# Layer 0 of a two-layer decoder trunk: all column chunks of w_in over four parts of K, with the attention moved behind them

## The chip, the cores and the metric

The kernel runs on one core of a Trainium2 chip. The metric is the device time of one execution in microseconds. The kernel before took 2464.14 us (median of 3 runs, 2459.02 to 2468.23).

## The reference

Two layers on 256 tokens of width 2048, all float32. A layer normalizes x, scales and shifts it by values that come from a vector c through `w_mod`, multiplies by `w_in` (2048 x 5900 columns), runs three kinds of attention over the projections (4 MoBA heads, 4 NSA heads with two softmax branches and one compressed branch each, 8 FoX heads), multiplies by `w_out`, and then runs an MLP of squared ReLU.

```
mod = silu(c) @ w_mod + b_mod           # six groups of 2048 columns a layer
h = rms_norm(x, g_pre_mix) * (1 + scale) + shift
p = h @ w_in                            # q, k, v of MoBA; q, k, v, gates of NSA; q, k, v, forget of FoX
o = concat(moba(p), nsa(p), fox(p))     # 16 heads of 128
x = x + gate * rms_norm(o @ w_out, g_post_mix)
x = x + gate2 * mlp(modulated rms_norm(x))
```

FoX adds to each score the running sum of log sigmoid(forget); the compressed branch of NSA runs k and v blocks of 32 tokens through a small MLP with a GELU first.

## The kernel before, in words

Every product is made of three TensorE products: ScalarE casts a weight block to a shortened float (`hi`, L233), VectorE subtracts to get the rest (`lo`, L234), and TensorE multiplies hi by hi, hi by lo and lo by hi (`gemm_b`, L238 to L252). The block is a `unit` (L221): one transfer of 4 K tiles of 128 rows by up to 512 columns, 1 MiB, and 24 matmuls of 128x512. `chunk_a` (L265) makes the transposed form for FoX's q and k, 64 pairs of matmuls, 16 for each unit. Weights arrive in a ring of four 1 MiB buffers (`raw`).

The modulation `w_mod` is 16 MiB for each of six groups a layer. `mod_chunk` (L120) does it in one of two ways: VectorE multiplies and adds 1024 columns at a time (L148), or TensorE multiplies 512 columns of four K tiles at once (L143) and VectorE or ScalarE sums the result (L150 to L152). `Spread` (L189) lets a step of this work follow after each unit or head, at a rate given by R0 or MO; `tick` (L209) does that, and steps of the NSA compression (`comp`) come before it. Where `ring` holds names of big buffers, the w_mod blocks go into them, otherwise they share `raw`. The instruction order of each engine is fixed when the kernel is built, and an engine takes its instructions strictly in that order.

Layer 0 has four parts of K (q = 0 to 3), so that TensorE starts when a quarter of h is there. In each part, two 512-column chunks add up in PSUM (`pq`), and six more chunks (1024, 2048, 1536 and three of 344 columns) rotate through two PSUM banks: `rotate` (L558) sums them in SBUF, by ScalarE copy in part 0 and VectorE add (L572) later. Modulation groups 1 and 0 are made on TensorE beside the parts. After the last part come the four MoBA heads, the chunk of 268 columns with the NSA compression, FoX q and k of four heads by `chunk_a`, 8 softmax heads of NSA, 4 FoX heads, FoX q and k of the other four, their heads, and `w_out` in two halves of two column chunks. The boundary to the MLP (residual, normalization, transposes) follows. Layer 1 uses whole chunks and no parts.

A head (`softmax_head` L423) is scores (L431, L434; FoX also L433, L436, L437), mask and maximum (L443, L445), exp (L447), gate or reciprocal, three transposes (L455), a copy to SBUF (L457) and the product with v (L461, L462), which `put_split` writes (L465, L466). `to_heads` (L468) turns a projected chunk into heads: copy or add, rope, transposes (L484), copy (L485). `compress` (L494) multiplies blocks of raw compression weights (L506), copies to `hp`, transposes them (L514), makes the GELU and multiplies by the second weights (L528).

Of the kernel before, what the change touches and what calls it, by code (L numbers as in the profile page):

```python
# [20 lines left out]
NC = 15  # L21
NEG = -1e30
PES = (0, 1)
R0 = 48.5
MO = (3,3,4,5,5,5,5)
ROT = 6
CB = True
EXTRA = (7,)
# [4 lines left out]
G0 = ((0, 4), (0, 2), (0, 3))  # L33
# [3 lines left out]
AFD = ()  # L37
HIA = False
RA = (("S3", 1), ("", 1))
RB = ()  # L40
# [6 lines left out]
def trunk(ctx, tc, x, c, positions, w_mod, b_mod, g_pre_mix, g_post_mix, g_pre_mlp, g_post_mlp, w_in, b_forget,  # L47
# [56 lines left out]
    for l in range(DEPTH):  # L104
        stage = wk.tile([128, 128], F32, tag="P", name="stage", bufs=3)
        dma(stage[:96], b_mod[l].rearrange("(r k) -> r k", k=128))
        tp = ps_t()
        T.transpose(tp[:, :96], stage[:96], ident[:96, :96])
        V.tensor_copy(bm[:, l], tp[:, :96])

# [98 lines left out]
    def tick(w=1.0):  # L209
        if w == 1.0 and comp[0] is not None:  # L210
            if next(comp[0], 0) is None:
                if CB:
                    return
            else:
                comp[0] = None
# [104 lines left out]
    def norm_tile(h, l, which, r, t, q):  # L320
# [6 lines left out]
        for j in range(4):  # L327
            k = 4 * q + j
            if j in AFD:
                last[1] = V.tensor_scalar(hf[:, j], tp[:, j * 128:(j + 1) * 128], ac[:, k:k + 1], sh[:, k:k + 1],  # L330
                                op0=OP.mult, op1=OP.add)
            else:
                last[0] = A.activation(hf[:, j], tp[:, j * 128:(j + 1) * 128], AF.Identity, bias=sh[:, k:k + 1],
                             scale=ac[:, k:k + 1])
        ht = h[q // 2][:, 4 * q % 8:4 * q % 8 + 4, :, t * 128:(t + 1) * 128]
        if HIA:
            A.copy(ht[:, :, 0], hf)
        else:
            V.tensor_copy(ht[:, :, 0], hf)
# [32 lines left out]
    posi = cp.tile([128, 2], I32, name="posi")  # L372
    dma(posi, positions.rearrange("b (t p) -> p (b t)", p=128))
    posf = cp.tile([128, 2], F32, name="posf")
    V.tensor_copy(posf, posi)
    ang = cp.tile([128, 2, 16], F32, name="ang")
    for t in range(2):
        V.tensor_scalar(ang[:, t], invf, posf[:, t:t + 1], None, op0=OP.mult)
    sc = cp.tile([128, 2, 2, 16], F32, name="sc")
    C1 = 6.28125  # L380
    C2 = 0.001934051513671875
    C3 = 2.0 * math.pi - C1 - C2
    PI = 3.1415925
    for i, off in enumerate((0.25, 0.0)):
# [523 lines left out]
```

## Time and profile before

| | |
|---|---|
| median of 3 runs | 2464.14 us |
| profiled execution, span | 2459.2 us |
| TensorE busy | 2376.0 us (97%) |
| VectorE busy | 1648.0 us (67%) |
| ScalarE busy | 1210.9 us (49%) |
| mean granted TensorE clock | 0.986 |

The span runs from the first instruction to the last of the one profiled execution; the median of the runs lies 4.9 us above it. In the trace, layer 0 starts its first w_in matmul at 44.9 us, leaves the third part at 209 us, and ends w_out at 535.5 us; the boundary to the MLP then lasts to 557 us. TensorE is busy nearly all the time, so a stretch is read by how much of it TensorE waits and by what it has to do in it.

### The profile page before, as it was taken

How to read it: one execution, taken by the hardware profiler on the slowest of the kernel's cores; microseconds unless marked ns; L12 is line 12 of the kernel's file. 1: busy time of each engine (PE TensorE's matmuls, PEld its weight loads, DVE VectorE, ACT ScalarE, POOL GpSimd, SP SyncE). 2: the span in 40 equal slices, each digit the busy share in tenths (PEclk: the TensorE clock that was granted, in tenths of full speed). 3: DMA queues.
4: the chain of work that ended last, by engine and by line, in shares of the span. 5: the costliest groups of instructions: out<-in, count | busy, mean ns of one | idle time of the engine just before them, and what ended most of it. 6: DMA issues, size and time to landing. Idle time of an engine off the chain costs nothing.

```text
span 2459.2 us, 32050 instructions
## 1 busy us (share of the span) xinstructions
PE 2376.0 (97%) x12444; PEld 1977.0 (80%) x12444; DVE 1648.0 (67%) x2255; ACT 1210.9 (49%) x2025; POOL 12.9 (1%) x20
## 2 busy tenths in 40 slices
PE   5999999989999999999989999999999999999998
PEld 3678777778888888888878879887788888888886
DVE  3459688887777777777668467765665665665555
ACT  3435454455545535535545455544654553553553
POOL 0000000000000000000000000000000000000000
PEclk8999999999999999999999999999999999999999
DMA  9788888987888888888657588865567666666553
GB/s 348 284 327 309 300 293 297 349 296 244 296 296 281 309 304 278 311 277 308 199 199 273 188 276 306 282 244 180 176 227 234 222 237 225 221 205 198 187 189 120
DMA packets 292120, 632.83 MB, mean 257 GB/s; under 512 B 10608, under 2 KB 44800, under 8 KB 291712
## 3 DMA queue, kind: packets, MB, share of 16 engines
q1 hardware_dynamic: 291968, 630.79, 74.3%
q8 instruction: 97, 1.59, 0.3%
q14 instruction: 55, 0.45, 0.1%
HBM read 628.65 MB, written 2.10 MB: 256 GB/s over the span
## 4 chain that ended last, share of the span: by engine, by line
PE 88%; DVE 4%; DMA 4%; ACT 2%; issue 1%; POOL 0%; SPq 0%; DVEq 0%; POOLq 0%; ACTq 0%
PE psg L276 17%; PE psg L248 14%; PE psg L249 14%; PE psg L250 14%; PE psg L278 8%; PE psu L276 6%; PE psu L278 3%; PE psr L249 2%; PE psr L250 1%; PE psr L248 1%; PE pst L143 1%; PE pst L177 1%; DMA raw<-in_w_in_dram 1%; PE pst L325 1%; DMA rawm<-in_w_mod_dram 1%
## 5 line engine op out<-in xcount | busy, mean ns | idle before, releaser
L234 DVE TENSOR_TENSOR lo<-raw,hi 128x1024 fp32r<-128x1024 f32 (+2 forms) x784 | 928.6, 1191 | 582.3 <-ACT hi L233 580.8
L233 ACT CAST hi<-raw 128x1024 fp32r<-128x1024 f32 (+2 forms) x784 | 798.5, 1026 | 923.6 <-PE psg L250 468.3
L276 PE MATMUL psg<-S,hi 128*128 128x512 f32 x1888 | 674.3, 398 | 1.5 <-ACT hi L233 1.2
L248 PE MATMUL psg<-hi,S 128*128 128x512 f32 (+2 forms) x1664 | 640.1, 386 | 3.4 <-ACT hi L233 1.8
L249 PE MATMUL psg<-lo,S 128*128 128x512 f32 (+2 forms) x1664 | 638.4, 384 | 1.2 <-DVE lo L234 1.2
L250 PE MATMUL psg<-hi,S 128*128 128x512 f32 (+2 forms) x1664 | 637.5, 383 | 1.1 <-DVE S L340 1.1
L278 PE MATMUL psg<-S,lo 128*128 128x256 f32 x1888 | 528.6, 282 | 1.1 <-DVE lo L234 1.1
L276 PEld LDWEIGHTS psg<-S,hi 128*128 128x128 f32 x1888 | 355.1, 188 | 86.4 <-ACT hi L233 2.3
L248 PEld LDWEIGHTS psg<-hi,S 128*128 128x128 f32 x1664 | 312.5, 188 | 69.8 <-issue 4.2
L249 PEld LDWEIGHTS psg<-lo,S 128*128 128x128 f32 x1664 | 313.2, 188 | 61.8 <-DVE lo L234 3.1
L250 PEld LDWEIGHTS psg<-hi,S 128*128 128x128 f32 x1664 | 313.0, 188 | 61.2 <-DVE S L340 2.1
L278 PEld LDWEIGHTS psg<-S,lo 128*128 128x128 f32 x1888 | 357.1, 189 | 4.8 <-DVE lo L234 2.9
L148 DVE SCALAR_TENSOR_TENSOR acc<-rawm,cact,acc 128x1024 f32<-128x1024 f32 x226 | 289.2, 1280 | 16.6 <-DMA rawm<-in_w_mod_dram 14.7
L276 PE MATMUL psu<-S,hi 128*128 128x512 f32 x672 | 244.1, 397 | 0.0
L278 PE MATMUL psu<-S,lo 128*128 128x256 f32 x672 | 188.2, 280 | 0.0
L276 PEld LDWEIGHTS psu<-S,hi 128*128 128x128 f32 x672 | 126.2, 188 | 30.9 <-ACT hi L233 0.2
L278 PEld LDWEIGHTS psu<-S,lo 128*128 128x128 f32 x672 | 126.8, 189 | 0.3 <-issue 0.2
L249 PE MATMUL psr<-lo,S 128*128 128x512 f32 (+1 forms) x192 | 69.7, 363 | 1.5 <-DVE lo L234 1.5
L248 PE MATMUL psr<-hi,S 128*128 128x512 f32 (+1 forms) x192 | 68.5, 364 | 0.8 <-ACT hi L233 0.8
L250 PE MATMUL psr<-hi,S 128*128 128x512 f32 (+1 forms) x192 | 69.0, 359 | 0.0
L812 ACT ACTIVATE xu<-xu 128x256 f32<-128x256 f32 x128 | 52.6, 412 | 26.1 <-DVE xu L811 26.1
L325 PE MATMUL pst<-dg,xt 128*128 128x128 f32 x256 | 45.0, 342 | 20.9 <-DVE dg L317 19.9
(186 smaller groups left out, 1545.4 us busy)
## 6 DMA issues: line engine op xcount, KB each, us to landing
raw<-in_w_up_dram SPq DMA_DIRECT2D x128, 1024.0 KB, 5.3
raw<-in_w_down_dram SPq DMA_DIRECT2D x128, 1024.0 KB, 5.2
rawm<-in_w_mod_dram SPq DMA_DIRECT2D x119, 1024.0 KB, 6.0
raw<-in_w_in_dram SPq DMA_DIRECT2D x72, 1024.0 KB, 6.8
S<-in_w_mod_dram SPq DMA_DIRECT2D x16, 2048.0 KB, 11.0
raw<-in_w_out_dram SPq DMA_DIRECT2D x32, 1024.0 KB, 6.2
X<-in_w_mod_dram SPq DMA_DIRECT2D x26, 1024.0 KB, 7.3
raw<-in_w_in_dram SPq DMA_DIRECT2D x24, 688.0 KB, 6.2
```

The costliest lines, as they stand in the source:

```text
L143: T.matmul(pm[32 * k:32 * k + 32], cs.to_broadcast([128, 32]), raw[:, k], start=True, stop=True, tile_position=(0, 32 * k))
L148: V.scalar_tensor_tensor(acc, raw[:, k], cs, acc, op0=OP.mult, op1=OP.add)
L177: T.matmul(ps[:, j:j + 1], acc[:, j * 128:(j + 1) * 128], ones[:, 0:1], start=True, stop=True)
L233: A.copy(hi[:, :, :w], r)
L234: V.tensor_tensor(lo[:, :, :w], r, f32(hi[:, :, :w]), OP.subtract)
L248: T.matmul(ps[t][:, :w], xh, hi, start=first, stop=False)
L249: T.matmul(ps[t][:, :w], xh, lo, start=False, stop=False)
L250: T.matmul(ps[t][:, :w], xl, hi, start=False, stop=last)
L276: T.matmul(ps[d], hi[:, kk, ws], a.rearrange("p s n -> p (s n)"), start=(u == 0 and h == 0 and kk == 0), stop=False)
L278: T.matmul(ps[d][:, :256], lo[:, kk, ws], a[:, 0], start=False, stop=last)
L325: T.matmul(tp[:, j * 128:(j + 1) * 128], xt[:, t, k * 128:(k + 1) * 128], r, start=True, stop=True)
L812: A.activation(u, u, AF.Relu)
```

## The change

- Layer 0 rotates four FoX q and k chunks (columns 2828 on, 512 each) and the 268-column chunk too, in all four parts; their sums are in a big buffer `F` (`fac`), in `ack` and `vn`. They use the plain form of `gemm_b` and are turned by `to_heads`, where `chunk_a` produced the transposed form directly.
- In the last part the order is: MoBA's q, k, v; the four FoX chunks into `M`; the MoBA heads; the chunks 2048 and 268; the gates; 1536 with the compression; three of 344; then NSA, the forget gate's logarithm, all eight FoX heads, and w_out.
- w_out walks K outside and the two column chunks inside, in both layers.
- Modulation groups 1 and 0 alone stand beside parts 0 to 2 (before, one unit of the rest was drawn in with each); groups 4, 2, 3 all follow from the last part on, and group 2 is made on TensorE.
- At the start, the first w_mod transfers are issued before those of biases, positions and tables, and the work for those follows the first modulation units.
- Layers have their own big tags (S0, S1, F, M); in layer 1 this is a renaming.

The core of the diff:

```diff
-    def mod_groups(*lg):
+    def mod_groups(*lg, pe=()):
         for l, g in lg:
-            for q in range(2):
-                yield from mod_chunk(l, g, q, 1024)
+            if g in pe:
+                for q in range(4):
+                    yield from mod_chunk(l, g, q, 512, pe=True)
+            else:
+                for q in range(2):
+                    yield from mod_chunk(l, g, q, 1024)
...
+            gen = mod_first(0, (("M", 2), ("F", 2), ("S1", 2), ("", 1), ("", 1)))
+            for _ in range(3):
+                next(gen)
+            load_biases()
+            next(gen)
+            dma(xt, x.rearrange("b (t p) d -> p (b t) d", p=128))
+            for _ in gen:
+                pass
+            load_tables()
...
                 if q < 3:
-                    spread[0] = Spread(mod_both(q + 1), 8 + len(EXTRA), MO[ROT])
+                    spread[0] = Spread(mod_first(q + 1, (("M", 2), ("S1", 2)) if q < 2 else (("M", 2), ("", 1), ("", 1))),
+                                       8, MO)
                 else:
-                    ring[0] = RA
-                    spread[0] = Spread(rest, 48 - 3 * len(EXTRA), R0)
+                    spread[0] = Spread(mod_groups((0, 4), (0, 2), (0, 3), pe=(2,)), 48, R0)
...
+                if q < 3:
+                    for i in range(4):
+                        rotate(q, 2828 + 512 * i, 512, [fac[:, i]])
+                    for i in range(2):
+                        rotate(q, (2048, 1536)[i], 512, [ac2[:, i]])
+                    rotate(q, 2560, 268, [ack[:, :, 0:128], vn[:, :, 640:768], ack[:, :, 128:140]])
+                else:
+                    qfm = big("M", [128, 2, 8, 256], F32)
+                    qfs.extend([qfm[:, 0], qfm[:, 1]])
+                    for i in range(4):
+                        kind, gr = i // 2, i % 2
+                        to_heads(rotate_last(2828 + 512 * i, 512), qfs[gr], range(4 * kind, 4 * kind + 4), None, acc=fac[:, i])
+                    oT.append(big(TS["o"][0], [128, 8, 2, 256]))
+                    moba()
+                    to_heads(rotate_last(2048, 512), qk, range(4, 7), slice(0, 3, 2), vcopy=[(vn[:, :, 512:640], 384, 128)],
+                             acc=ac2[:, 0])
+                    ps = rotate_last(2560, 268)
...
+                    gate_values([ack[:, t, 128:140] for t in range(2)])
+                    comp[0] = compress_both(l, qk, load_w2(), cres)
+                    to_heads(rotate_last(1536, 512), qk, range(0, 4), slice(0, 4), acc=ac2[:, 1])
+                for i in range(3):
+                    rotate(q, 4876 + 344 * i, 344, [vt[:, :, 688:1024], lf] if i == 2 else [vt[:, :, 344 * i:344 * i + 344]])
...
+            ring[0] = RA
+            nsa()
+            log_forget()
+            ring[0] = ()
+            oT.append(big(TS["o"][1], [128, 8, 2, 256]))
+            fox_attn(0)
+            fox_attn(1)
...
         for pair in range(2):
             pp = [[ps_g(), ps_g()] for _ in range(2)]
-            for i in range(2):
-                for u in range(3):
+            for u in range(3):
+                for i in range(2):
                     gemm_b([(otile, Wo, 4 * u, 4 * u, (2 * pair + i) * 512, 512, pp[i], u == 0, False)])
```

In the changed kernel the same operations carry other lines: the three products are L236 to L238, hi L221, lo L222, TensorE's w_mod L128, VectorE's w_mod L133, a head's operations L423 to L458, the compression L498, L506, L520, and the add of `rotate` L667.

The order of TensorE at the first compression, before. L506 is a compression group, L514 the transposes of its result, L276 and L278 the FoX matmuls of `chunk_a`.

```order
L506 MATMUL pst<-rawc,tx 16x256 x8
L514 MATMUL pst<-cst,hp 128x15 x2
L276 MATMUL psg<-S_149,hi 128x512 x4
L278 MATMUL psg<-S_149,lo 128x256
L276 MATMUL psg<-S_149,hi 128x512
L278 MATMUL psg<-S_149,lo 128x256 x2
L276 MATMUL psg<-S_149,hi 128x512
```

The same place after. L498 is the compression group, L506 the transposes of its result, L520 the second weights, L580 the compressed scores, L423 the first NSA head's scores.

```order
L238 MATMUL psr<-hi,S_1446 128x344
L498 MATMUL pst<-rawc,tx 16x256 x8
L506 MATMUL pst<-cst,hp 128x15 x2
L520 MATMUL pst<-xg,w_2734 128x15 x2
L498 MATMUL pst<-rawc,tx 16x256 x32
L580 MATMUL spc<-kcmp,X_117 128x15 x8
L423 MATMUL pss<-X_117 128x128
L426 MATMUL pss<-X_117 128x256
```

What stood beside the compression of k and v (FoX matmuls) now stands far ahead of it; the k chain's three steps follow each other, then the groups of v, then NSA.

The order of TensorE in the FoX heads, before: L455 are a head's transposes, L461 its product with v, L276 and L278 the FoX matmuls of the second group.

```order
L276 MATMUL psg<-S_149,hi 128x512
L455 MATMUL pst<-cst,P 128x128
L278 MATMUL psg<-S_149,lo 128x256
L276 MATMUL psg<-S_149,hi 128x512
L455 MATMUL pst<-cst,P 128x128 x2
L278 MATMUL psg<-S_149,lo 128x256
L276 MATMUL psg<-S_149,hi 128x512
L278 MATMUL psg<-S_149,lo 128x256
L276 MATMUL psg<-S_149,hi 128x512
L461 MATMUL pst<-PT,X_160 128x256
```

After, in the FoX heads: L447 are the transposes, L453 and L454 the product with v, L423 to L429 the next scores, L128 modulation group 2.

```order
L128 MATMUL pst<-rawm,cact 32x512 x4
L429 MATMUL pss<-cst,lu 128x256
L447 MATMUL pst<-cst,P 128x128 x3
L423 MATMUL pss<-M 128x128
L453 MATMUL pst<-PT,X_119 128x256
L454 MATMUL pst<-PT,X_119 128x128
L128 MATMUL pst<-rawm,cact 32x512 x4
L425 MATMUL pss<-cst,lu 128x128
L426 MATMUL pss<-M 128x256
```

Between a head's steps there are now scores of the next head and a modulation group; matmuls of a weight unit come only at the last head, 9 of the 384 of w_out.

The order of VectorE in the MoBA heads, before: L443 and L445 are mask and maximum, L148 the modulation, L234 the `lo` of a weight unit.

```order
L443 ISA P,mx<-pss,cst 128x128
L443 ISA mx 128x1
L443 ISA P,mx<-pss,cst 128x256
L443 ISA mx 128x1
L234 TENSOR_TENSOR lo<-raw,hi 128x2x268
L445 TENSOR_SCALAR mx<-mx 128x2
L148 SCALAR_TENSOR_TENSOR acc<-S_1958,cact,acc 128x1024
L443 ISA P,mx<-pss,cst 128x128
L443 ISA mx 128x1
L148 SCALAR_TENSOR_TENSOR acc<-S_1958,cact,acc 128x1024
```

After: L435 and L437 are mask and maximum, L133 the modulation, L440 the reciprocal, L458 the write of a head, L222 the `lo` of the 2048 chunk.

```order
L435 ISA P,mx<-pss,cst 128x128
L435 ISA mx 128x1
L133 SCALAR_TENSOR_TENSOR acc<-rawm,cact,acc 128x1024
L458 TENSOR_TENSOR F<-pst,F 128x256
L435 ISA P,mx<-pss,cst 128x256
L435 ISA mx 128x1
L133 SCALAR_TENSOR_TENSOR acc<-rawm,cact,acc 128x1024
L440 RECIPROCAL sm<-sm 128x2
L437 TENSOR_SCALAR mx<-mx 128x2
L133 SCALAR_TENSOR_TENSOR acc<-rawm,cact,acc 128x1024
L458 TENSOR_TENSOR F<-pst,F 128x256
L222 TENSOR_TENSOR lo<-raw,hi 128x1024
```

Before, a `lo` of the next weight unit came among the second head's operations; now it comes at the end of the third, behind seven modulation operations (L133).

## Rows read from the trace of the kernel before

**Rows 1.** Busy times by stretch; columns named in its second line
```profile
core 0 of [0], span 2459.2 us
core 0: us, PE busy (x) PEld busy (x) DVE busy (x) ACT busy (x) POOL busy (x), PEclk, DMA share, GB/s
44.90:209.00 164.10, 158.39 (x866) 116.89 (x867) 91.68 (x124) 63.93 (x98) 0.00 (x0) 0.99 0.85 306
209.00:253.10 44.10, 44.08 (x238) 37.54 (x236) 42.34 (x78) 21.05 (x30) 0.00 (x0) 1.00 0.84 308
253.10:268.50 15.40, 13.71 (x89) 11.82 (x89) 14.49 (x43) 11.20 (x36) 0.00 (x0) 1.00 0.98 330
280.00:283.00 3.00, 0.69 (x16) 0.12 (x4) 1.70 (x12) 2.96 (x9) 0.00 (x0) 0.99 1.09 353
283.00:286.50 3.50, 3.39 (x9) 2.40 (x10) 2.25 (x7) 2.24 (x4) 0.00 (x0) 0.50 1.06 377
342.90:370.90 28.00, 22.52 (x126) 16.38 (x124) 26.20 (x92) 21.11 (x68) 0.00 (x0) 1.00 0.83 301
428.00:535.50 107.50, 103.53 (x484) 84.65 (x484) 88.35 (x116) 48.05 (x82) 0.55 (x1) 1.00 0.94 344
```

**Rows 2.** Timeline, start: us, duration, engine, line, out<-in, count, idle before
```profile
4.54 0.38 SPq L134 DMA_DIRECT2D S<-in_w_mod_dram  x1
...
34.61 3.64 PE L143 MATMUL pst<-S,cact 128*32 128x512 f32 x16 [1.77 <-DMA S<-in_w_mod_dram]
```

**Rows 3.** Timeline of TensorE inside a part of K
```profile
96.81 0.32 PE L248 MATMUL psr<-hi,S 128*128 128x344 f32 x1
...
101.26 0.32 PE L250 MATMUL psr<-hi,S 128*128 128x344 f32 x1
...
107.73 1.06 PE L143 MATMUL pst<-S,cact 128*32 128x512 f32 x8
...
109.29 0.40 PE L250 MATMUL psg<-hi,S 128*128 128x512 f32 x1
...
114.07 0.39 PE L250 MATMUL psg<-hi,S 128*128 128x512 f32 x1
```

**Rows 4.** Lines by form: count, busy us, mean ns, idle before and releaser
```profile
L234 DVE TENSOR_TENSOR lo<-raw,hi 128x1024 fp32r<-128x1024 f32 x720 | 876.7, 1223 | 556.6 <-ACT hi L233 555.2 <-PE pst L462 0.4
...
L148 DVE SCALAR_TENSOR_TENSOR acc<-rawm,cact,acc 128x1024 f32<-128x1024 f32 x226 | 289.2, 1280 | 16.6 <-DMA rawm<-in_w_mod_dram 14.7
...
L177 PE MATMUL pst<-cst,acc 128*128 128x1 f32 x256 | 31.1, 249 | 4.9 <-DVE acc L152 4.9
...
L484 PE MATMUL pst<-cst,ev 128*128 128x128 f32 x64 | 10.7, 279 | 1.0 <-DVE ev L407 0.8
...
L572 DVE TENSOR_TENSOR X<-psr,X 128x512 f32<-128x512 f32 x6 | 4.1, 689 | 2.8 <-PE psr L250 2.8
```

**Rows 5.** Timeline of ScalarE: table loads between the softmax of MoBA and the gates
```profile
269.00 1.28 ACT L744 ACT_TABLE_LOAD   x1
...
279.81 1.28 ACT L676 ACT_TABLE_LOAD   x1
```

**Rows 6.** Timeline of the first compression
```profile
279.63 1.06 PE L506 MATMUL pst<-rawc,tx 128*16 128x256 f32 x16
...
283.07 1.03 PE L514 MATMUL pst<-cst,hp 128*128 128x15 f32 x4 [2.38 <-ACT hp L511]
...
289.56 0.61 PE L528 MATMUL pst<-xg,w 128*128 128x15 f32 x4
```

**Rows 7.** Timeline of ScalarE: copies that end a head's transposes
```profile
348.87 0.48 ACT L457 COPY PT<-pst 128x384 f32<-128x384 f32 x1 [0.52 <-PE pst L455]
...
367.89 0.46 ACT L457 COPY PT<-pst 128x384 f32<-128x384 f32 x1
...
436.06 0.48 ACT L457 COPY PT<-pst 128x384 f32<-128x384 f32 x1 [0.53 <-PE pst L455]
...
448.74 0.48 ACT L457 COPY PT<-pst 128x384 f32<-128x384 f32 x1
```

More of the change, by code (lines that the diff above doesn't have):

```diff
@@ L103, in trunk @@
     bm = cp.tile([128, DEPTH, 96], F32, name="bm")
[L104 to L109, printed above, removed]
     xt = cp.tile([128, 2, D], F32, name="xt")
@@ L328, in norm_tile @@
             k = 4 * q + j
[L329 to L334, printed above, removed]
+            last[0] = A.activation(hf[:, j], tp[:, j * 128:(j + 1) * 128], AF.Identity, bias=sh[:, k:k + 1],
+                                   scale=ac[:, k:k + 1])
         ht = h[q // 2][:, 4 * q % 8:4 * q % 8 + 4, :, t * 128:(t + 1) * 128]
[L336 to L339, printed above, removed]
+        V.tensor_copy(ht[:, :, 0], hf)
         V.tensor_tensor(ht[:, :, 1], hf, f32(ht[:, :, 0]), OP.subtract)
@@ L396, in trunk, with load_biases @@
-    A.activation(sc, sc, AF.Sin)
+    sc = cp.tile([128, 2, 2, 16], F32, name="sc")
+    peT = cp.tile([128, 2, DEPTH, 32], F32, name="peT")
+    bfg = cp.tile([128, DEPTH * 8], F32, name="bfg")
+    def load_biases():
+        for l in range(DEPTH):
+            stage = wk.tile([128, 128], F32, tag="P", name="stage", bufs=3)
+            dma(stage[:96], b_mod[l].rearrange("(r k) -> r k", k=128))
+            tp = ps_t()
+            T.transpose(tp[:, :96], stage[:96], ident[:96, :96])
+            V.tensor_copy(bm[:, l], tp[:, :96])
@@ L680, in trunk @@
-        gt = gates.rearrange("p t (h b) -> p b h t", b=3)
-        V.tensor_tensor(gv, gt[:, 0], valid[:, None, :].to_broadcast([128, 4, 2]), OP.mult)
-        if l or ROT < 3:
+            comp[0] = compress_both(l, qk, w2, cres)
+            ps = chunk_b(act, W, 2560, 268)
+            to_heads(ps, qk, range(7, 8), slice(0, 1), vcopy=[(vn[:, :, 640:768], 128, 128)])
+            gate_values([ps[t][:, 256:268] for t in range(2)])
             ps = chunk_b(act, W, 1536, 512)
             to_heads(ps, qk, range(0, 4), slice(0, 4))
-        early = not l and ROT == 6
@@ L686, in trunk @@
-        if early:
-            fox_group(0)
-        for _ in comp[0] or ():
-            pass
-        comp[0] = None
-        kcmp, vcmp = cres
-        sp = pss.tile([128, 4, 2, NC], F32, tag="s", name="spc")
-        for h in range(4):
-            for t in range(2):
-                T.matmul(sp[:, h, t], qk[:, h, t * 128:(t + 1) * 128], kcmp, start=True, stop=True)
-        pc = wk.tile([128, 8, NC], F32, tag="pc", name="pc", bufs=1)
-        V.tensor_tensor(pc, sp.rearrange("p h t c -> p (h t) c"), cmask.rearrange("p (a c) -> p a c", c=NC), OP.add)
@@ L723, in trunk @@
-        ring[0] = RB
-        done = 0 if l else max(0, ROT - 3)
-        if l:
-            lf = st.tile([128, 2, 8], F32, tag="lf", name="lf", bufs=1)
-        if not done:
+            nsa()
+            ring[0] = ()
             vt = big("X4", [128, 2, 1024], F32)
-        if done < 3:
-            for i in range(done, 3):
+            for i in range(3):
                 ps = chunk_b(act, W, 4876 + 344 * i, 344)
@@ L780, in trunk @@
             pp = [[ps_g(), ps_g()] for _ in range(2)]
-            for i in range(2):
-                for u in range(3):
+            for u in range(3):
+                for i in range(2):
                     gemm_b([(otile, Wo, 4 * u, 4 * u, (2 * pair + i) * 512, 512, pp[i], u == 0, False)])
```

376 lines of the change are left out of this document (184 added, 192 removed).

## The prediction

> **What bounds the kernel now.** I read the stretches of layer 0 first, since MLP and layer 1 are left as they are but for names of buffers and the order of w_out. In the three first parts of K TensorE is busy 158.4 of 164.1 us, in the last part 44.1 of 44.1, and from 428 us to the end of w_out 103.5 of 107.5 [rows 1]. VectorE has 117, 42 and 88 us there, and DMA is at 0.84 to 0.94. So TensorE's content sets the pace, with two places of another kind: the MoBA heads (15.4 us, VectorE busy 14.5) and the NSA heads (28.0 us, VectorE 26.2, TensorE 22.5). There a chain from engine to engine, with VectorE in it, sets the pace. The forecast therefore counts TensorE where weight units stand, and chains where heads stand without them.
>
> Prices: a 512-column matmul every 0.228 us (109.29 to 114.07, 21 steps), so 24 for a unit, 5.46; a 344-column one every 0.153 (96.81 to 101.26, 29 steps), unit 3.68 [rows 3]; a 268-column unit 2.87 by columns (my estimate between the two). A modulation group of four matmuls on TensorE 1.06, a VectorE modulation step 1.28, a `lo` 1.22, a sum 0.69, a transpose 10.7/64 = 0.17 [rows 3, 4].
>
> **The change part by part.** All to the end of w_out, 535.5 before in the profiled execution of 2459.2 us; the median lies 4.9 above that span, and I add the same.
>
> Start. The first w_mod transfer is issued at 4.54 and the modulation's last group takes 3.64 just before the matmuls begin [rows 2]. Four small transfers, at some 0.4 of issue each (0.38 in the row), move behind, and smaller w_mod blocks let the last group be half as long (1.8). The sine and its table work now come later, about 0.5 of it on the path. 44.9 becomes 41.9; bounds 40.5 to 44.9, the latter if the whole start waits for bytes, which DMA share 0.85 next door allows.
>
> Parts 0 to 2. Before: 15 units of 5.46, 9 of 3.68 and 24 modulation groups are 140.4 of the 164.1 us; 23.7 are normalization, transposes, waits. After: 27 units of 5.46, three of 2.87, nine of 3.68 and 24 groups are 214.5. The 23.7 stays, less 4.9 in which the modulation's transposes waited for its sum (L177) [rows 4]: they now have units on both sides. That gives 233.3, an end at 275. Five more chunks a part are copied by ScalarE in part 0 and summed by two adds (0.69) in parts 1 and 2, on VectorE at 0.56 busy; half of the next unit's matmuls (2.7 us) hides an add, as for the six chunks now. Were one add or copy of each new chunk late, it would be 15 times 0.69, +10. Bounds 228 to 243.
>
> Last part, front: seven units 38.2 and 48 transposes 8.0, 46.2 on TensorE; VectorE has 14 `lo`, 13 modulation steps, 10 sums, ropes, about 44.6, nearly as much. I take 47.5 (46.2 to 52). End 322.4.
>
> MoBA heads. TensorE's content is about 12. On VectorE, the heads' own work is 14.5 less four modulation steps and a small `lo` of 0.7, 8.7. In the new order seven modulation steps stand between the first head's masks and the first `lo` of the next unit, and two more around it: 8.7 + 9 times 1.28 + 1.2 = 21.4. The unit's matmuls queue behind that `lo`, and the last head behind the steps. I take 21 (12 if the steps have slipped ahead since their data is early, 24 if their data is late). End 343.4.
>
> Units 2048's rest, 268, 1536, three of 344, 16 transposes and three compression groups are 26.3 of TensorE; I take 28 (26 to 32). End 371.4.
>
> Compression. Before, the third step of k comes 6.5 us after the second begins (283.07 to 289.56), with FoX matmuls between them; the wait for the copies alone is 2.38 [rows 6]. Now nothing stands there: group 1.06, wait 2.38, transposes 1.03, GELU chain about 3.5, and the four groups of v 4.2, is 12.2; I take 12 (8 if the copies come early, 16 with the clock below). End 383.4. This is the cost of an edit that seems free: the FoX matmuls, moved into the parts, were the cover.
>
> At this place the clock counts: TensorE was busy 0.69 of the 3 us from 280 to 283, and in the next 3.5 its granted clock was 0.50, the lower of its two levels (1.2 GHz) [rows 1]. I charge nothing separate for it in the 12, up to 3.5 in the bound. The Trainium skill, "TensorE: Matmul & The Clock Gate" ("Why this matters for your kernels"), has idle gaps of TensorE bring back the low clock. The stretch at 342.9, with 5.5 us of idle spread over 28, stayed at 1.00, so here it is one long gap and not many short ones that costs. By the rule the new gap in the k chain and the filling before the first NSA head would each cost a stretch at 0.50, 3.5 more than my sum.
>
> The k chain also holds the forget gate's exp and logarithm: two table loads of 1.28 stand there in ScalarE's order. Before, a load stood at the logarithm (269.00) and another at the next exp (279.81) [rows 5]. The Trainium skill, "ScalarE: Activation LUTs" ("Table sets: the hidden batching unit"), says that logarithm and exp share a set, so that one load would serve both; the trace shows a load each way. By the rule the chain would be 1.28 shorter; I go by the rows.
>
> Heads of NSA and FoX, 16 softmax heads. Before, eight NSA heads followed each other at 2.72 us (348.87 to 367.89, 7 steps) after a filling of 6.0 from 342.9; the last four FoX heads at 4.2 (436.06 to 448.74, 3 steps) with FoX matmuls among them [rows 7]. Now all 16 stand without weight units, but with twelve modulation groups and with VectorE's modulation. I choose 3.5, between, nearer to the NSA row since most of the filler is gone: FoX has two more matmuls a head and the groups 12.7 in all. 6 + 16 times 3.5 = 62 (49 at 2.72, 73 at 4.2). End 445.4. TensorE has 55 in there.
>
> w_out. 16 units 87.4, four groups 4.2, 16 modulation transposes at 31.1/256 = 0.12 [rows 4] 2; waits as in the stretch at 428, 4 in 107 us [rows 1]; start 1.4: 99 (95 to 106). End 544.4. The inner loop over column chunks needs four PSUM banks at once, as before; in layer 1 the same swap moves nothing on the path, 0 (-1 to +2).
>
> So 544.4 instead of 535.5, +8.9; boundary and the rest as before: 2464.1 + 8.9 = 2473. Read as content: TensorE gains 17 for group 2 (16 groups of 1.06), 5 for the transposes, and waits move. The FoX matmuls that used to cover chains in the attention are now in the parts, where TensorE was full already, and the order doesn't weave w_out with the heads: 9 of its 384 matmuls stand before the last head's product.
>
> **The rivals.** First, faster: the chains keep their price without filler. The NSA row, at 2.72 with VectorE full, speaks for it: heads 49.5 instead of 62, and MoBA 12 instead of 21 when its modulation steps run ahead. That is 21.5 less, 2451.5, and with a start or a compression 2 us shorter, 2449. Against it: modulation steps of 1.28 are in VectorE's order between the masks, and in the NSA row VectorE had no time to spare.
>
> Second, slower: heads at the FoX price. It is one mechanism: TensorE's order puts the next head's scores and a modulation group ahead of each product, so that a late w_mod block or sum stops the chain. At 4.2 instead of 3.5, 16 heads cost 11 more, and the MoBA heads 4 more by the same blocks: 2488. It decides from 3.55 a head on, where the sum passes +9.7. For it speaks that the shared four-buffer ring now serves w_mod and w_out in the attention.
>
> Third, DMA. From 275 to 544 there are 11.5 MiB of w_in, 16 of w_out, 48 of w_mod and 8 of compression, 83.5 MiB or 87.6 MB, less 4.2 in flight; at 306 GB/s, the rate in the parts, 272.5 us, at 301, the rate in the heads, 277, while the sum gives 269.5. Stretches at 330 and 344 [rows 1] speak against it. It costs 3 to 8: 2476 to 2481, say 2481.
>
> That the change does not do what it says is true of the weaving, and is in the sum.
>
> **How the numbers follow.** Half a percent, 12.3 us, is about what a measurement here can tell from no change: same is 2451.8 to 2476.5. Forecast 0.46, its own range 2463 to 2483, of which 0.34 is same and 0.12 slower. Faster rival 0.18, of which 0.15 is faster. Heads slower 0.24, of which 0.21 slower. DMA 0.12, of which 0.09 slower. Faster 0.15, same 0.43, slower 0.42. The range takes in most of both sides, 2448 to 2495.
>
> **What would show it.** The third part ends at about 275; if after 285, the sums are not hidden; if before 268, TensorE's waits in the parts were the removed ones. MoBA takes about 21 us with VectorE busy and TensorE not; near 12, the steps ran ahead. The k chain shows a gap of 2 to 6 us on TensorE with a granted clock of 0.50 behind it. Copies of a head's transposes follow at 3.5 in the attention. w_out takes 99 us with TensorE full; if TensorE waits there for DMA, the third rival holds. The forecast is wrong if MLP or layer 1 move by more than 3 us.

## The result

The changed kernel takes 2520.51 us (median of 4 runs, 2515.81 to 2523.95) against 2462.01: ratio 1.0232, interval 1.0215 to 1.025. It is slower by 58 us where 9 were forecast. The stretches of its profiled execution (span 2522.2), with the columns of [rows 1]:

```profile
core 0 of [0], span 2522.2 us
core 0: us, PE busy (x) PEld busy (x) DVE busy (x) ACT busy (x) POOL busy (x), PEclk, DMA share, GB/s
44.50:280.50 236.00, 233.88 (x1208) 177.77 (x1209) 130.31 (x173) 94.56 (x130) 0.00 (x0) 0.99 0.76 264
280.50:331.80 51.30, 47.99 (x246) 38.98 (x245) 42.32 (x60) 22.34 (x34) 0.00 (x0) 1.00 0.83 291
331.80:350.70 18.90, 13.97 (x62) 9.94 (x60) 17.45 (x41) 14.89 (x38) 0.00 (x0) 0.82 0.67 216
350.70:383.50 32.80, 30.44 (x215) 24.15 (x214) 23.27 (x66) 9.75 (x19) 0.00 (x0) 1.00 0.94 306
383.50:398.30 14.80, 9.81 (x89) 5.84 (x89) 2.62 (x18) 6.13 (x13) 0.00 (x0) 0.65 0.83 274
398.30:476.50 78.20, 67.94 (x359) 41.87 (x359) 39.61 (x166) 40.74 (x127) 0.00 (x0) 0.89 0.65 220
476.50:595.20 118.70, 107.67 (x460) 80.96 (x459) 88.47 (x87) 38.38 (x53) 0.55 (x1) 0.94 0.93 338
...
403.00:408.00 5.00, 3.51 (x20) 2.14 (x18) 5.00 (x12) 2.93 (x11) 0.00 (x0) 1.00 0.45 172
408.00:413.00 5.00, 4.36 (x19) 3.75 (x19) 1.92 (x11) 2.68 (x9) 0.00 (x0) 0.63 0.61 201
413.00:418.00 5.00, 5.00 (x20) 3.95 (x20) 1.35 (x7) 1.39 (x5) 0.00 (x0) 0.50 0.59 222
...
500.00:560.00 60.00, 54.24 (x232) 42.73 (x231) 51.83 (x47) 19.72 (x26) 0.00 (x0) 0.97 0.99 366
```

Stretch by stretch against the forecast: start 44.5 (41.9 forecast), parts 0 to 2 236.0 (233.3), front and MoBA heads 70.2 (68.5), units 32.8 (28), compression 14.8 (12), heads of NSA and FoX 78.2 (62), w_out 118.7 (99). That is 51 us over the sum, 36 of them in the last two. The boundary takes 22.1 (21.5 before), and after it the two profiled executions differ by another 2.5 us: of the 63.0 us between them, layer 0 up to the end of w_out holds 59.7.

Two things are to be seen in the last rows. In the heads DMA stood at 0.65 and 220 GB/s, VectorE was half idle, and the granted clock was 0.89. In w_out DMA was at 0.93, and at 0.99 and 366 GB/s from 500 to 560. So bytes that were not fetched in the heads were fetched in w_out.

The same, parted at the last head's product. The first line is the kernel before, from there to the end of w_out; the others are the changed kernel, from the compressed scores to the last head's product and from there to the end of w_out:

```profile
450.20:535.50 85.30, 85.22 (x391) 70.53 (x390) 66.84 (x66) 34.45 (x46) 0.55 (x1) 1.00 0.93 338
...
396.50:483.40 86.90, 75.88 (x410) 47.11 (x410) 43.59 (x171) 44.98 (x136) 0.00 (x0) 0.90 0.65 218
483.40:595.20 111.80, 101.53 (x430) 77.52 (x429) 84.49 (x82) 35.60 (x48) 0.55 (x1) 0.94 0.96 348
```

Behind the last head, w_out took 85.3 us before and takes 111.8 now, at nearly the same rate. Rate times length is 28.8 MB before and 38.9 MB now; 11 blocks of w_mod are issued there before, 18 now. ScalarE, which makes `hi`, waits there for the weights of w_out (before, then after; us in total, times, longest):

```profile
ACT hi L233 <- DMA raw<-in_w_out_dram: 26.7, 8, 4.6
...
ACT hi L221 <- DMA raw<-in_w_out_dram: 58.1, 14, 8.4
```

Before, no wait of TensorE is left behind the last head.

The first compression on TensorE, answering to [rows 6]: L506's transposes, L520 the second weights, L498 the groups of v.

```profile
382.43 1.06 PE L498 MATMUL pst<-rawc,tx 128*16 128x256 f32 x16
385.13 0.77 PE L506 MATMUL pst<-cst,hp 128*128 128x15 f32 x4 [1.65 <-ACT hp L503]
389.25 1.04 PE L520 MATMUL pst<-xg,w 128*128 128x15 f32 x4 [3.36 <-DVE xg L516]
390.22 6.32 PE L498 MATMUL pst<-rawc,tx 128*16 128x256 f32 x64
```

ScalarE between 385 and 389:

```profile
385.33 1.28 ACT L615 ACT_TABLE_LOAD   x1
...
386.86 1.28 ACT L513 ACT_TABLE_LOAD   x1
```

The step from L506 to L520 takes 4.1 us, near the forecast's 4.5, and holds a table load for the logarithm and one for the next exp. TensorE waits 1.65 and 3.36, and the four groups of v behind that take 6.3 where I had 4.2: the clock was down (0.65 over the stretch).

The first and the last of the 16 copies that end a head's transposes, answering to [rows 7]:

```profile
405.19 0.48 ACT L449 COPY PT<-pst 128x384 f32<-128x384 f32 x1 [1.28 <-PE pst L447]
...
481.91 0.48 ACT L449 COPY PT<-pst 128x384 f32<-128x384 f32 x1 [3.60 <-PE pst L447]
```

A head every 5.11 us (76.72/15), not 3.5. The waits of the queue that issues transfers in the heads, then the longest sum of TensorE's own in the heads, and last those of TensorE in w_out (us in total, times, longest):

```profile
SPq L119 <- PE pst L128: 40.5, 8, 12.9
...
SPq L151 <- DVE gg L155: 5.4, 2, 5.2
```

```profile
PE pst L453 <- ACT PT L449: 3.8, 7, 0.6
```

```profile
PE psg L237 <- DVE lo L222: 5.7, 7, 2.1
PE pst L162 <- DVE acc L133: 3.6, 1, 3.6
PE psg L236 <- ACT hi L221: 1.6, 3, 1.1
```

L119 issues w_mod, and it waits 40.5 of 78.2 us for TensorE's modulation matmul (L128) to give its buffer back. That matmul stands about once a head in TensorE's order, so w_mod comes at about one block of 1 MiB a head, and w_out's weights wait behind it in the same queue. TensorE itself waits in the heads for the copies that end a head's transposes more than for anything else, and none of its waits there names a transfer of w_mod. In w_out it then waits for `lo` and `hi`, behind which stands DMA, as the waits of ScalarE show, and once for VectorE's modulation sums (L133).

### The profile page after: what moved, and what is told of

It is laid out like the page before. It is cut to its first block, busy times and chain, and to the rows that moved or that the text cites. A ratio compares the mean times of both kernels' runs of the same rounds, so it can differ in the third digit from the quotient of the medians.

```text
span 2522.2 us, 32170 instructions
## 1 busy us (share of the span) xinstructions
PE 2422.1 (96%) x12476; PEld 1986.5 (79%) x12476; DVE 1634.1 (65%) x2261; ACT 1220.7 (48%) x2031; POOL 12.2 (0%) x20
## 4 chain that ended last, share of the span: by engine, by line
PE 86%; DVE 5%; DMA 5%; ACT 2%; issue 1%; POOL 0%; SPq 0%; DVEq 0%; POOLq 0%; ACTq 0%
PE psg L264 14%; PE psg L237 13%; PE psg L238 13%; PE psg L236 13%; PE psg L266 7%; PE psu L264 6%; PE psu L266 3%; PE psr L236 3%; PE psr L237 3%; PE psr L238 3%; PE pst L128 2%; DMA raw<-in_w_out_dram 1%; DVE lo L222 1%; DMA rawm<-in_w_mod_dram 1%; PE pst L162 1%
## 5 line engine op out<-in xcount | busy, mean ns | idle before, releaser
L222 DVE TENSOR_TENSOR lo<-raw,hi 128x1024 fp32r<-128x1024 f32 (+2 forms) x784 | 929.4, 1190 | 623.3 <-ACT hi L221 621.8
L221 ACT CAST hi<-raw 128x1024 fp32r<-128x1024 f32 (+2 forms) x784 | 799.9, 1026 | 992.2 <-PE psg L238 478.0
L236 PE MATMUL psg<-hi,S 128*128 128x512 f32 x1024 | 403.0, 395 | 5.2 <-ACT hi L221 4.0
L237 PE MATMUL psg<-lo,S 128*128 128x512 f32 x1024 | 401.4, 392 | 1.6 <-DVE lo L222 1.6
L238 PE MATMUL psg<-hi,S 128*128 128x512 f32 x1024 | 400.3, 391 | 0.6 <-DVE S L321 0.6
L133 DVE SCALAR_TENSOR_TENSOR acc<-rawm,cact,acc 128x1024 f32<-128x1024 f32 x210 | 268.8, 1280 | 34.7 <-DMA rawm<-in_w_mod_dram 32.8
L264 PE MATMUL psg<-F,hi 128*128 128x512 f32 x816 | 291.1, 397 | 0.0
L236 PEld LDWEIGHTS psg<-hi,S 128*128 128x128 f32 x1024 | 193.3, 189 | 49.3 <-ACT hi L221 5.9
L266 PE MATMUL psg<-F,lo 128*128 128x256 f32 x816 | 228.6, 280 | 0.0
L237 PEld LDWEIGHTS psg<-lo,S 128*128 128x128 f32 x1024 | 193.5, 189 | 44.3 <-DVE lo L222 3.9
L238 PEld LDWEIGHTS psg<-hi,S 128*128 128x128 f32 x1024 | 193.5, 189 | 41.0 <-DVE S L321 1.0
L264 PEld LDWEIGHTS psg<-F,hi 128*128 128x128 f32 x816 | 153.1, 188 | 36.9
L264 PE MATMUL psg<-M,hi 128*128 128x512 f32 x480 | 173.0, 400 | 1.8 <-DVE xu L824 1.8
L236 PE MATMUL psg<-hi,M 128*128 128x512 f32 (+2 forms) x400 | 153.0, 383 | 1.4 <-DVE rv L272 1.3
L266 PEld LDWEIGHTS psg<-F,lo 128*128 128x128 f32 x816 | 154.0, 189 | 0.1
L238 PE MATMUL psg<-hi,M 128*128 128x512 f32 (+2 forms) x400 | 152.5, 381 | 0.2 <-DVE M L321 0.2
L236 PE MATMUL psr<-hi,S 128*128 128x512 f32 (+2 forms) x352 | 131.3, 373 | 0.0
L238 PE MATMUL psr<-hi,S 128*128 128x512 f32 (+2 forms) x352 | 127.7, 363 | 0.0
```

Source lines behind the costliest of these rows:

```text
L133: V.scalar_tensor_tensor(acc, raw[:, k], cs, acc, op0=OP.mult, op1=OP.add)
L221: A.copy(hi[:, :, :w], r)
L222: V.tensor_tensor(lo[:, :, :w], r, f32(hi[:, :, :w]), OP.subtract)
L236: T.matmul(ps[t][:, :w], xh, hi, start=first, stop=False)
L237: T.matmul(ps[t][:, :w], xh, lo, start=False, stop=False)
L238: T.matmul(ps[t][:, :w], xl, hi, start=False, stop=last)
```

## The experiments

Theory A: w_mod's bytes come late, and w_out pays. Theory B: the heads have lost the cover of weight units. All ratios are against the kernel before, differences against 2520.5. The four runs of the changed kernel lie up to 8.1 us apart, so a difference of a few us is not told from none.

**Modulation drawn into the parts; w_out woven into the heads; group 2 on VectorE**

```diff
 early_mods
+            rest = mod_groups((0, 4), (0, 3), (0, 2), pe=(2,))
+            def mod_both(q, tags):
+                for i, _ in enumerate(mod_first(q, tags)):
+                    yield
+                    if i % 2:
+                        next(rest)
+                        yield
...
-                    spread[0] = Spread(mod_groups((0, 4), (0, 2), (0, 3), pe=(2,)), 48, R0)
+                    spread[0] = Spread(rest, 36, 30.0)
 weave, in fox_attn, with u, i counting over w_out's first units
+                if not l and h in (0, 1, 2, 3, 5, 6):
+                    gemm_b([(otile, Wo, 4 * u, 4 * u, i * 512, 512, pp0[i], u == 0, False)])
 group2_vector
-                    spread[0] = Spread(mod_groups((0, 4), (0, 2), (0, 3), pe=(2,)), 48, R0)
+                    spread[0] = Spread(mod_groups((0, 4), (0, 2), (0, 3)), 48, R0)
```

> Against the changed kernel (2520.5): 12 of the 48 steps of the remaining modulation are drawn into the first three parts of K (one after every second step of groups 1 and 0), and group 2, on TensorE, comes last instead of second. Theory A (late w_mod bytes): in the changed kernel 20 MiB of w_mod stand beside w_out's 16 MiB in 118.7 us at 338 GB/s, so w_out waits for bytes; with 12 MiB moved into the parts, where DMA was at 226 to 288 GB/s, w_out falls from 118.7 to about 100 and the total to about 2503; the parts stay within 4 us. Theory B (missing cover): the loss lies in the heads and in gaps of TensorE that no weight unit covers, and w_out's length follows from its own start; then w_out stays over 112 and the total over 2514.

2510.75, ratio 1.0195 (1.0175 to 1.0215), 10 less, between the totals that the two theories had. Parts, then w_out behind the last head's product (in the changed kernel 111.8):

```profile
44.70:287.10 242.40, 235.22 (x1225) 179.67 (x1226) 155.95 (x197) 93.95 (x130) 0.00 (x0) 0.99 0.85 305
...
484.90:583.50 98.60, 95.33 (x433) 71.03 (x432) 51.61 (x55) 37.83 (x50) 0.55 (x1) 1.00 0.84 287
```

The parts take 242.4, 6 more, with DMA at 305 GB/s instead of 264; w_out takes 98.6, a fall of 13 where theory A had 18 and B next to none, and the total gains less because the parts pay. The run also puts group 2 last, so it does not tell what the early bytes gave w_out from what the order of the groups gave.

> Against the changed kernel: six units of w_out's first half (K parts 0 to 2 of two column chunks) are emitted among the FoX heads, one behind each of six heads, so that they really stand between the heads on TensorE. Theory B (missing cover): the heads of NSA and FoX wait 10 of 78.2 us and run part of it at the lower clock; with weight units there, the time from the first NSA head to the end of w_out (196.9 us) falls by 12 to 20. Theory A (bytes): the same bytes must come in the same stretch, at 220 GB/s in the heads before, now more evenly; it falls as well, by the share of w_out's waits, about 10 to 15, but w_out's remaining ten units still run at over 6.5 us each. So total 2500 to 2510 by both; what tells them apart is the price of a remaining w_out unit (5.5 by B, over 6.5 by A).

2517.18, ratio 1.0218 (1.0198 to 1.0239), 3 less, which is not told from none; both theories had 10 to 20. The six units do stand among the heads, but the other ten take 71.9 us, 7.2 each:

```profile
516.70:588.60 71.90, 64.52 (x273) 51.19 (x272) 57.38 (x57) 24.47 (x37) 0.55 (x1) 0.93 0.92 334
```

By the price of a unit, set before the run, that is A and not B.

> Against the changed kernel: modulation group 2 goes back to VectorE (1024 columns a step), the order of groups as in the changed kernel. TensorE loses 16 groups of 1.06 us, VectorE gains 32 steps of 1.28. If the modulation groups between a head's steps on TensorE are what lengthens the heads (4.9 us each), the heads get shorter by about 10 us and the total falls to about 2508. If the heads are bound by the chain through VectorE, the 41 us of steps lengthen them, and the total is 2520 to 2535.

2514.27, ratio 1.0207 (1.0191 to 1.0223), 6 less, between the two that were expected. The heads:

```profile
395.60:479.20 83.60, 65.70 (x315) 49.18 (x312) 69.94 (x192) 43.96 (x133) 0.00 (x0) 0.88 0.73 254
```

TensorE has 17 us less to do, and the heads still take 83.6 behind the compressed scores (86.9 in the changed kernel): neither engine is a cheap place for group 2 there.

> Both of the edits early_mods and weave. If A and B are separate losses they add: about 2485 to 2492. If they are two views of one loss (bytes that come late because the heads hold the queue up), the sum is little better than the better of the two, 2498 to 2505.

2500.19, ratio 1.0151 (1.0134 to 1.0167), 20 less, more than 10 and 3, and in the range that was expected of one loss seen twice. What is left of w_out behind the last head:

```profile
520.10:573.70 53.60, 52.38 (x229) 42.32 (x227) 29.92 (x33) 22.50 (x35) 0.55 (x1) 1.00 0.78 265
```

These are 228 matmuls, 9.5 units, 5.6 us each: once the bytes come early, weaving pays.

**Cover and clock**

```diff
 cover_344: the last part's three units of 344 columns, called behind NSA heads' first branches
-                for i in range(3):
+                for i in range(3 if q < 3 else 0):
+            nsa([lambda i=i: rotate(3, 4876 + 344 * i, 344, ..., ps_g) for i in range(3)])
 warm: n = 5 ahead of L506, 12 behind it, 6 behind each branch of two NSA heads
+                        for _ in range(n):
+                            T.matmul(dm, o[:, 0, :128], o.rearrange("p a b -> p (a b)"), start=True, stop=True)
```

> Against the changed kernel (2520.5): the last part's three 344-column units are emitted among the NSA heads, in PSUM banks that are free there, so that their 72 matmuls stand in the order beside the compression's k chain and the first NSA heads. Theory B (cover): gaps of 1.65, 3.36, 0.76 and 1.26 us in the compression and the first heads close, and the lower clock that followed them (0.65 in the compression, 0.50 in 413 to 423) goes: 6 gained in the gaps, up to 10 in the clock, total 2505 to 2512. Rival A (w_mod bytes late): the time saved comes back as waits of w_out, which moves no earlier than its bytes; total within 4 of 2520.

2535.27, ratio 1.0306 (1.0275 to 1.0337), 15 more: both were wrong. The compressed scores come 17 us earlier (379.3 for 396.5, with 11.5 of units moved behind), but the heads then lose it. TensorE's longest wait there:

```profile
PE pst L162 <- DVE acc L133: 7.6, 1, 7.6
```

Modulation transposes (L162) stand ahead of a head's transposes in TensorE's order; their sums wait for w_mod, which waits in the queue behind a unit's transfer, and that waits 7.6 us for its buffer. Here, cover that needed bytes was no cover.

> Against the changed kernel: idle TensorE is given 41 matmuls of 128x512 on finished data, whose result nobody reads, in the compression's k chain and around the first two NSA heads. They do no useful work (41 x 0.227 = 9.3 us if all stood on the path), so only the granted clock can gain. If the clock after the gaps is a cost of its own, the stretch from the end of the w_in units to the last head's product runs at over 0.95 instead of 0.65 and 0.89, and the total falls by 3 to 8. If it is not, the total rises by 0 to 9.

2512.41, ratio 1.0204 (1.0182 to 1.0226), 8 less, with 41 matmuls more; all four runs (2511.35 to 2513.39) lie below those of the changed kernel. The mean granted clock is 0.986 instead of 0.981. From the 268-column units to the compressed scores, and the heads:

```profile
350.00:391.20 41.20, 39.49 (x308) 30.66 (x307) 24.16 (x80) 14.04 (x27) 0.00 (x0) 1.00 0.91 298
391.20:474.90 83.70, 71.85 (x411) 44.58 (x407) 43.55 (x171) 44.52 (x135) 0.00 (x0) 0.94 0.71 235
```

In the changed kernel the two stretches take 45.8 and 86.9. The clock stayed at 1.00 through the compression. So in this order the lower clock costs time of its own.

> All of: modulation drawn into the parts, w_out units among the FoX heads, 344 units among the NSA heads, and group 2 on VectorE. early_weave gave 2500.2. If the cover's 6 to 10 us and TensorE's 17 us of group 2 come off, 2475 to 2485; if VectorE (32 more steps, 41 us) becomes the bound in the attention, 2490 to 2500.

2517.49, ratio 1.0225 (1.0202 to 1.0249), over both that were expected: the cover spoils early_weave as it spoiled the changed kernel. The same edit without the cover, early_weave_vector below, takes 2497.60.

```diff
 before_k_outer
-            for i in range(2):
-                for u in range(3):
+            for u in range(3):
+                for i in range(2):
```

> The kernel before with nothing changed but w_out's loops, K outside and column chunks inside, in both layers. By all theories it costs nothing: within 3 us of before. If it costs 5 or more, part of the loss belongs to this swap.

2461.14, ratio 0.9997 (0.9987 to 1.0008): the swap in w_out costs nothing in the kernel before.

**What of w_mod made it long**

```diff
 without_group3
-                    spread[0] = Spread(mod_groups((0, 4), (0, 2), (0, 3), pe=(2,)), 48, R0)
+                    spread[0] = Spread(mod_groups((0, 4), (0, 2), pe=(2,)), 32, R0 * 32 / 48)
+                    V.memset(modc[:, 0, 2], 0.0)
 mod_rate_28
+                    spread[0] = Spread(mod_groups((0, 4), (0, 3), (0, 2), pe=(2,)), 48, 28.0)
 group3_one_block
-                dma(wide, w_mod...)
+                if not once or u == 0:          # once: layer 0, group 3; wide is then one kept block
+                    dma(wide, w_mod...)
 group3_load_only
+                    n = 8 if (l, g) == (0, 3) else w
+                    V.scalar_tensor_tensor(acc[:, :n], raw[:, k, :n], cs, acc[:, :n], op0=OP.mult, op1=OP.add)
 bare_heads
+                    spread[0] = Spread(mod_groups((0, 4)), 16, R0 / 3)
+                    V.memset(modc[:, 0, 2], 0.0)
...
+            V.memset(gg_cell[0], 1.0)
```

> Leaves out layer 0's modulation group 3 (16 MiB of w_mod and 32 steps of VectorE, whose result is set to zero); the other 32 steps keep their rate. It is all that stands beside w_out in the changed kernel. Theory A (bytes): w_out's waits for weights and modulation (11 us idle, 7 us at the lower clock) go: from the last head's product to w_out's end 111.8 falls to 90 to 95, total 2498 to 2504. If w_out's length is its own (its order, its banks, its clock), the fall is under 8.

2495.74, ratio 1.0128 (1.0112 to 1.0144), 25 less; w_out behind the last head takes 89.1 (row below). That is what theory A had, and a little more. It leaves out group 3's steps with its bytes; the two runs after the next part them.

> Against the changed kernel: the 48 modulation steps spread over 28 instead of 40 units of work, groups in the order 4, 3, 2 (group 2 on TensorE last), nothing moved into the parts. It pulls bytes out of w_out's stretch into the heads, where DMA was at 220 GB/s. Theory A: w_out falls by 10 or more and, as the heads wait for chains and not for bytes, they rise by less; total 2505 to 2514. Rival: the heads' in-order queues carry the steps (1.28 each on VectorE, between masks), so what w_out gains the heads lose; total 2517 to 2525.

2550.08, ratio 1.0348 (1.0319 to 1.0377), 30 more: both expectations were too low. From the compressed scores to the last head's product:

```profile
411.60:516.70 105.10, 79.78 (x395) 53.37 (x392) 62.16 (x186) 43.28 (x133) 0.00 (x0) 0.77 0.73 251
```

105.1 us at a clock of 0.77. VectorE ahead of TensorE's longest wait there (4.09 us, ended by the mask at 462.55):

```profile
458.36 1.28 DVE L133 SCALAR_TENSOR_TENSOR acc<-S,cact,acc 128x1024 f32<-128x1024 f32 x1
...
459.89 1.27 DVE L133 SCALAR_TENSOR_TENSOR acc<-rawm,cact,acc 128x1024 f32<-128x1024 f32 x1
...
461.16 0.27 DVE L435 CUSTOM_DVE_ANT_0 P<-pss,cst 128x128 f32<-128x128 f32 x1
...
461.35 1.28 DVE L133 SCALAR_TENSOR_TENSOR acc<-rawm,cact,acc 128x1024 f32<-128x1024 f32 x1
462.55 0.42 DVE L435 CUSTOM_DVE_ANT_0 P<-pss,cst 128x256 f32<-128x256 f32 x1
```

The scores for this mask were done at 459.0, and its two parts (L435) stand behind three modulation steps (L133). w_out gained 8 of its 112; the heads lost 18, and the stretch before them 15. The run changes the order of the groups with the rate, so the heads hold 23 modulation steps of VectorE where the changed kernel has 4: it prices steps between masks, and not bytes alone.

> Against the changed kernel: group 3 of layer 0 keeps its 32 VectorE steps, but loads one block per half of its columns and uses it for all steps (2 MiB instead of 16; this leaves out the product with the other rows). If bytes made w_out long: like without_group3, 2495 to 2502, w_out behind the last head 89 to 95. If the steps did: 2514 to 2521, w_out 106 to 112.

> Against the changed kernel: group 3 of layer 0 loads all its 16 MiB, but each VectorE step but the first works on 8 of its 1024 columns (this leaves out the other columns' sums). If bytes made w_out long: 2514 to 2521. If the steps did: 2495 to 2502.

2503.46 (ratio 1.0178, 1.0155 to 1.0201) without the bytes, 2514.96 (1.0218, 1.0203 to 1.0234) without the steps. w_out behind the last head, 111.8 in the changed kernel:

```profile
481.50:576.80 95.30, 95.26 (x440) 75.33 (x438) 67.61 (x69) 37.75 (x49) 0.55 (x1) 1.00 0.71 245
```

```profile
481.80:589.00 107.20, 99.89 (x431) 76.30 (x430) 53.55 (x83) 35.93 (x48) 0.55 (x1) 0.95 0.98 362
```

The first total lies 1.5 above what was expected of bytes, the second within it. Bytes are worth 16.5 us of w_out, steps 4.6, and both, as left out above, 22.7. (Without the bytes all 384 of w_out's matmuls stand behind the last head, in the others 372; at 0.228 the 12 are 2.7 us, so like for like the bytes are worth 19.) With the bytes there, DMA is at 0.98 and TensorE at a clock of 0.95; without, at 0.71 and 1.00.

> Against the changed kernel: leaves out layer 0's modulation groups 2 and 3 (set to one and zero), so that nothing of w_mod stands beside the NSA and FoX heads and w_out. w_out falls to about 90 as without_group3. If modulation between the heads' steps is what made them long, the stretch from the compressed scores to the last head's product falls from 86.9 to about 62 (forecast's 3.5 a head without its 12.7 us of groups would be 49); if it is their own chain without cover, it stays over 72. Totals 2467 to 2472 and 2480 to 2486.

2458.84, ratio 0.9984 (0.9975 to 0.9993), below both totals that were expected. The heads with w_out behind them, and the first and the last of the 16 copies:

```profile
395.90:453.80 57.90, 55.55 (x327) 44.32 (x324) 38.24 (x161) 45.64 (x137) 0.00 (x0) 1.00 0.40 137
453.80:531.60 77.80, 77.80 (x342) 63.75 (x340) 41.47 (x41) 31.46 (x41) 0.55 (x1) 1.00 0.63 208
```

```profile
404.62 0.48 ACT L449 COPY PT<-pst 128x384 f32<-128x384 f32 x1 [1.29 <-PE pst L447]
...
452.30 0.47 ACT L449 COPY PT<-pst 128x384 f32<-128x384 f32 x1
```

A head every 3.18 us, at a clock of 1.00. So the heads' own chain without cover is cheap, and theory B falls as the reason of the heads' length. Against without_group3, the same stretch is 84.3 there; the last line counts the matmuls of modulation (L128) alone:

```profile
397.50:481.80 84.30, 74.29 (x410) 46.56 (x410) 43.64 (x171) 44.85 (x135) 0.00 (x0) 0.92 0.67 226
481.80:570.90 89.10, 89.10 (x398) 70.29 (x398) 48.83 (x50) 37.66 (x49) 0.55 (x1) 1.00 0.78 265
...
397.50:481.80 84.30, 14.79 (x108) 2.15 (x112) 0.92 0.67 226
```

Group 2 made the stretch 26.4 longer. The cut at the last head hides a part of it: in bare_heads 42 matmuls of w_out stand ahead of that cut, in without_group3 12, and the 30 between are 6.8 us at 0.228. So like for like the heads are 33.2 longer and w_out, with three groups and two products of the gate (4.1 us), 4.5. In the heads, thirteen and a half groups take 14.8 and three products of the gate (L153) 3.3; TensorE's idle time rose from 2.4 to 10.0, and a clock of 0.92 costs at most 6.7 of 84.3.

> bare_heads with the idle matmuls of warm in the compression and the first NSA heads. If the lower clock lengthens the heads, 4 to 8 less than bare_heads; if not, 0 to 6 more.

2456.38, ratio 0.9974 (0.9964 to 0.9983), 2.5 less than bare_heads, which is neither of the two that were expected. The compressed scores come 3.6 us earlier (392.3 for 395.9), and the heads then run at 0.95 where bare_heads had 1.00: what the clock is worth without modulation stays open.

> early_weave (2500.2) with the idle matmuls of warm. If the clock's cost is separate from the bytes', it gives 4 to 8 again: 2492 to 2496. If early_weave has already closed those gaps, 2499 to 2503.

> early_weave (2500.2) with group 2 on VectorE, without the idle matmuls. early_weave_warm was 4 slower than early_weave, so the same edit without them should give 2496.8 - 4 = 2493, range 2490 to 2497.

> The last one with group 2 on VectorE. TensorE loses 16 groups of 1.06 us, VectorE gains 41 us of steps, in a stretch (the heads) where it was busy half of the time. If TensorE's content is the pace: 2480 to 2487. If the steps on VectorE delay masks and sums as much: 2492 to 2500.

2504.11, 2497.60 and 2496.83 (ratios 1.0162, 1.015, 1.0132); the first two lie just over what was expected. Idle matmuls on top of early_weave cost 4 instead of gaining, though the compressed scores came 2.3 earlier (400.0 for 402.3) and the clock ahead of them was 1.00 instead of 0.72: the heads behind them lost it again. So the 8 of warm is no price that carries over. Group 2 on VectorE gives 3 to 7. None comes near the kernel before: 2496.8 is the best complete version of the changed kernel, and the kernel before stays the faster.

## Why the prediction was wrong

The step that failed is the sum's heads and w_out, "I choose 3.5, between, nearer to the NSA row" and "99 (95 to 106)", together with the third rival, "It costs 3 to 8". All three take w_mod as so many instructions of so many microseconds and so many bytes over 269 us. The runs showed that its place was the cost: leaving out groups 2 and 3 gives 62 us back (2520.5 to 2458.8), more than the whole loss, while group 2 has 17 us of matmuls. The kernel before without these groups was not run. Its TensorE, from the last part of K to the end of w_out:

```profile
209.00:535.50 326.50, 310.88 (x1731) 253.75 (x1729) 264.24 (x480) 154.36 (x312) 0.55 (x1) 0.99 0.88 315
```

It is idle for 15.6 us there. With some 5 for the products of the groups' sums on TensorE, I estimate that it could gain 20, and that some 40 of the 62 belong to the place that the groups have in the changed kernel.

- Heads: the price without modulation was right. Of the 57.9 in bare_heads, 42 matmuls of w_out are 9.6, and the 48 that are left are what the NSA row's 2.72 a head gives (49). With modulation a head takes 5.11. I had twelve groups of 1.06 for it; group 2 adds 33.2 us, as worked out at bare_heads: 14.8 for the groups, 3.3 for products of its gate that the sum left out, 7.6 of idle time, and at most 6.7 for the clock.
- w_out: I counted TensorE's 93.6 and waits as before. There 18 blocks of w_mod fell beside 14 of weights, where before it was 11 beside 13: the NSA and FoX heads drew in about a block each, and by the order the steps of the compression take the place of w_mod's. The rate did not rise with the bytes (338 and 348 GB/s). The third rival named DMA, but as a mean over all stretches, where a fast stretch makes good a slow one. A queue that stands still in the heads can't do so.
- Clock: "I charge nothing separate for it". It was 0.65 in the compression, 0.89 in the heads and 0.94 in w_out, where before it was 1.00 from 342.9 to the end of w_out. What the clock lacks to 1.00, times the length, adds up to 20.9 us over these three stretches, an estimate from above, since a TensorE that waits loses nothing; warm gave 8 back. (The mean over the whole execution says little: it is 0.981 here and 0.982 in bare_heads.) After 403 to 408, with TensorE busy 3.51 of 5 us, the clock fell to 0.50 and was still there at 413 to 418, with TensorE busy 5.00 of 5; it was at 1.00 at 423. The rule that I weighed from the Trainium skill, "TensorE: Matmul & The Clock Gate" ("Why this matters for your kernels"), that idle gaps bring back the low clock, held at both places named (0.65 over the compression, 0.50 behind the gap in the first heads). My 3.5 for it was on the low side. My reading that one long gap costs, and not many short ones, did not hold in the first heads: TensorE's longest wait there was 1.26 us (up to 407.90).
- Compression, parts and MoBA: right within 3 us each (12 to 14.8, 233.3 to 236.0, 21 to 18.9; the last part's front 4 too short, 47.5 to 51.3, and the units behind MoBA 5, 28 to 32.8). The start gained 0.4 where 3 were forecast: its last transposes do end 3.6 earlier (40.7 for 44.3), but TensorE then waits 3.77 for the first `hi`: ScalarE, held up by the table load and the sine that the edit moved to 40.24, casts it only at 43.41. Right was also the reading that the swap in w_out costs nothing and that the order does not weave (by the trace 12 of w_out's matmuls stand ahead of the last head's product, not 9). weave and early_weave show that weaving as such gains only when the bytes are early.
- The table loads: two of 1.28 in the k chain, as the order had it; the rule on shared sets in the Trainium skill, "ScalarE: Activation LUTs" ("Table sets: the hidden batching unit"), does not describe this program, which loads anew for logarithm and exp.
- The second rival ended on the right side (2488), but the trace does not bear out its reason, a late w_mod block or sum that stops the chain: no wait of TensorE in the heads names a transfer of w_mod, and those for modulation's sums and bias are 2.4 us in all. Its price, 4.2 a head, was a row with other filler. That it decides from 3.55 a head on was a slip: by the band of 12.3 us it is 3.71.

What stays open: of group 2's 37 us (2495.7 to 2458.8), 33 are in the heads and 4 or 5 in w_out, but how much of the heads' idle time is due to the order on TensorE and how much to the small transfers of its bias and gate (5.4 us of waiting at L151; the chain that ended last holds one for the bias, 5.06 us from 437.95) was not tried apart.

## What to carry to other kernels

Count the bytes of each stretch against its own time, not of the whole: a background stream that the order ties to a slow chain, one block a step, comes late and is paid for where the next stream of weights is. Before moving weight work out of an attention, ask what the background work behind it will then wait for; and price a filler instruction in a chain of heads with all that comes along with it, its sums, the idle time and the clock, not by its own length. Put background loads where the transfers have time to spare (here 0.76 in the parts, though early_mods paid 6 of w_out's 13 there), and charge the clock for each gap that loses its cover.

## What was not expected of the hardware

The lower clock outlasted the gap by far: after one gap at 406 us TensorE ran at 0.50 for some ten microseconds although it was busy all the time, with transposes, scores and a modulation group that took 1.94 us there and 1.06 elsewhere. The slice behind those shown above:

```profile
418.00:423.00 5.00, 5.00 (x16) 2.28 (x17) 1.24 (x9) 2.89 (x9) 0.00 (x0) 0.50 0.00 2
```

And 41 matmuls that compute nothing made the changed kernel 8 us faster, while on early_weave the same 41 made it 4 slower.
